# A decoder trunk with product-key expert retrieval: query weights loaded by head, gated one-hot rows in fours of tokens

## The chip, the cores and the metric

One core of a Trainium2 chip runs the whole kernel in one launch. The metric is the device time in microseconds, the median of the runs shown; less is better.

## What is computed

Two residual layers over 256 tokens of width 1024, in float32: a gated short convolution, then a PEER channel mixer; MoBA attention (one block here), then a second PEER mixer. The PEER mixer is what the change touches:

```python
q = (xc @ w_q).reshape(PEER_CHUNK, PEER_HEADS, 2, PEER_HALF)
s1 = jnp.einsum('thd,nd->thn', q[:, :, 0], sub_k1)
s2 = jnp.einsum('thd,nd->thn', q[:, :, 1], sub_k2)
v1, i1 = lax.top_k(s1, PEER_TOPK); v2, i2 = lax.top_k(s2, PEER_TOPK)
...  # the best 16 of the 16 x 16 sums give e_idx; their softmax gives g
a = jax.nn.gelu(jnp.einsum('td,thkd->thk', xc, u_emb[e_idx]), approximate=False)
return jnp.einsum('thk,thkd->td', g * a, v_emb[e_idx])
```

There are 8 heads, 16 experts a head and token, and 128 x 128 experts.

## The kernel before

Instead of gathering, the kernel multiplies every token by all 16,384 rows of `peer_u` (128 items of 128 experts), weighs the gelu of that with a dense matrix of gates, and multiplies by all of `peer_v` (128 items). Each float32 operand is split in two, a rounded part `hi` and a rest `lo`, and three products are summed (hi by `XH`, hi by `XL`, lo by `XH`).

**Items.** All weights come through one line of items (`items`, 512 KB each, numbered over the whole kernel). SP loads an item into one of three `raw` tiles; for a `peer_u` item DVE turns it into `tr` (L145); ACT rounds it to `hi` (L156); POOL takes the difference `lo` in two halves for `peer_u` (L160), DVE mostly for other items; PE multiplies. Every one of `raw`, `tr`, `hi`, `lo` has three buffers, so nothing runs more than three items ahead. `next_item` (L205) writes the preparation of the items ahead first, then item n's matmuls, then side work. The query weights are 8 items of 128 rows each (`wap`, L83): the query of every head is complete only behind the eighth (`mm_wstat`, L423), and is then copied to `qT` in `xbuf` (L736). An U item is 24 matmuls of 256 columns (`u_mm`, L858).

**Side work.** The search and the gates are a list of small steps, each with a cost; behind each item `run_side(budget)` (L167) writes as many as the budget pays (1.62 for a U item). This fixes the order of every engine when the program is built. The list holds: the scores of the queries (L738, PE and a copy by ACT); the top 16 by MAX, MAX_INDEX and MATCH_REPLACE on DVE (L744); the folding of indices; `listed` (L808), which turns the lists; and then, for each of 32 groups of 8 tokens, the dense gates:
- `hots` (L886): DVE compares an iota with the indices and writes two one-hot tiles of 8 tokens (`OH2`, which alternates, and `OH1`);
- `gated` (L891): two DVE instructions multiply `OH1` by the gate's two float16 parts into `OHG`;
- a product (L897): 16 small matmuls (L901) write the 128 x 128 gates of each token to PSUM, two groups deep. `prod()` writes them at the end of the next U item's matmuls, or when the next `gated` or `mult` comes first;
- `mult` (L905): ACT copies the gates of the tiles that come later into `A` (L909), and DVE multiplies the tiles that are done (L911).
`out_pair` (L834) is the gelu of every second U item (ACT, L841 and L849), with a later DVE product (L845) for the tokens whose gates came first. All side work must be written before the last U item (`u_last`).

Below, the U items of a layer are numbered 0 to 127. In the program before, U items 69 to 121 lie beside the groups; this is called the one-hot stage, and U items 0 to 68 the search stage.

Of the kernel before, what the change touches and what calls it, by code (L numbers as in the profile page):

```python
# [21 lines left out]
T = 256  # L22
# [13 lines left out]
def trunk_kernel(ctx: ExitStack, tc, x, norm_mix, norm_ffn, conv_w_in, conv_w, conv_w_out,  # L36
# [29 lines left out]
    OH1, OHG = OH[:, 1], OH[:, 3:5]  # L66
    eT = sb.tile([128, T // TOK, 2, TOK // 2, 2], F16, name="eT")
    gT2 = sb.tile([128, T // TOK, 2, TOK // 2, 2], F16, name="gT2")
# [10 lines left out]
    def scratch(off, n):  # L79
        return big[:, off:off + n]  # L80
# [17 lines left out]
    def peer_items(l):  # L98
        for b in range(8):
            items.append(("w", wap(peer_w_q, l * D, D, 0, b)))  # L100
# [585 lines left out]
    def peer(l):  # L686
        base = 95 * 256
        S = scratch(base, 4096).rearrange("p (b h s n) -> p b h s n", b=2, h=8, s=2)
        qT = xbuf[:, 0:2048].rearrange("p (h t) -> p h t", t=256)
# [23 lines left out]
        U0 = state["use"] + 8  # L713
# [17 lines left out]
        pause(3)  # L731
        add(0.0, keys)
        for b in range(8):
# [21 lines left out]
        n = 0  # L755
        for i in range(2):
            for h in range(0, 8, 2):
                add(0.6, score, i, h, hi4[n % 4])
                n += 1
# [10 lines left out]
        for i in range(2):  # L770
            for h in range(0, 8, 2):
                topk([(S[:, i, h + a, s], v16[:, i, h + a, s], i16[:, i, s, h + a])
                      for a in range(2) for s in range(2)], 0.3)
            add(0.6, dve.tensor_copy, if16[:, i], i16[:, i])
# [45 lines left out]
        gates = lists[2].rearrange("p (s b t) -> p s b t", b=TOK // 2, t=2)  # L820
# [5 lines left out]
        st = {"tiles": 0, "toks": 0, "prod": None, "late": None, "listed": False}  # L826
# [25 lines left out]
        def prod():  # L852
            f, st["prod"] = st["prod"], None
            if f:
                f()
                credit[0] += 1.1

        def u_mm(k):  # L858
            def f(hi, lo):
                bk = lo4[(k // 2) % 4]  # L860
                o = bk[:, (k % 2) * 256:(k % 2) * 256 + 256]
                for b in range(8):
                    s = slice(b * 128, b * 128 + 128)
                    pe.matmul(o, hi[:, s], XH[:, b], start=(b == 0), stop=False)  # L864
                    pe.matmul(o, hi[:, s], XL[:, b], start=False, stop=False)  # L865
                for b in range(8):
                    s = slice(b * 128, b * 128 + 128)
                    pe.matmul(o, lo[:, s], XH[:, b], start=False, stop=(b == 7))  # L868
                if k % 2:
                    out_pair(k // 2, bk)  # L870
                prod()
            return f

        def g_side():
# [16 lines left out]
            def gated(s):  # L891
                prod()
                for a in range(2):
                    dve.tensor_tensor(OHG[:, a], OH1,  # L894
                                      gT2[:, s, a, :, None].to_broadcast([128, TOK // 2, 128, 2]), op=OP.mult)

                def f():  # L897
                    for t in range(TOK):
                        o = hi4[s % 2 * 2 + t // 4][:, t % 4 * 128:t % 4 * 128 + 128]
                        for a in range(2):  # L900
                            pe.matmul(o, OH2[s % 2][:, t // 2, :, t % 2], OHG[:, a, t // 2, :, t % 2],  # L901
                                      start=(a == 0), stop=(a == 1))
                st["prod"] = f

            def mult(s):  # L905
                prod()
                n, t = st["tiles"], slice(s * TOK, s * TOK + TOK)
                if n < NK:
                    act.activation(A[:, n:NK, t], tk(s, n, NK), AF.Copy)  # L909
                w = A[:, 0:n, t]  # L910
                dve.scalar_tensor_tensor(w, tk(s, 0, n), 1.0 / GSC, w, op0=OP.mult, op1=OP.mult)  # L911
                st["toks"] += TOK

            for s in range(NG + 1):
                if s < NG:
                    add(1.25, hots, s)
                    add(1.35, gated, s)
                if s >= 1:
                    add(0.9, mult, s - 1)
# [127 lines left out]
```

## Time and profile before

| | us |
|---|---|
| median of 3 runs (1925.06 to 1937.4) | 1932.14 |
| the profiled execution | 1938.75 |
| its span | 1936.9 |
| TensorE busy in it | 1836.0 |

A row of the trace gives an instruction or a group by its line, engine, operation and tiles; the idle time is that of the engine just ahead of it, with what ended it. PE's weight loads (PEld) lie beside its matmuls.

### The profile page before, as it was taken

To read this page: it belongs to the slowest core of one execution; us is meant where nothing else is said; L and a number is where in the kernel's file an instruction comes from. 1 tells how busy PE (TensorE), PEld (TensorE's weight loads), DVE (VectorE), ACT (ScalarE), POOL (GpSimd) and SP (SyncE) were. 2 spreads that over 40 slices of the span, in tenths; PEclk is the share of its full clock that TensorE was granted. 3 is DMA by queue.
4 is the path that set the end of the run, shared out by engine and by line. 5 is a ranking of instruction groups with operands and counts; after the bars stand their busy time and mean duration, and the time that the engine had idled before them with its cause. 6 is when DMAs were issued, how large, how long until landed. Compare 5 with 4: busy or idle time off the path is not lost.

```text
span 1936.9 us, 32437 instructions
## 1 busy us (share of the span) xinstructions
PE 1836.0 (95%) x12095; PEld 1671.4 (86%) x12095; DVE 1352.6 (70%) x2025; ACT 882.9 (46%) x1143; POOL 840.4 (43%) x561
## 2 busy tenths in 40 slices
PE   7999999888899999999999999998888899999998
PEld 7989999888799888888788799998888898888886
DVE  4757898888987555555554468988889885555555
ACT  4345545433335454544445455454333354544443
POOL 2227999867771000000163368989678720000000
PEclk9999999988999999999899999999899899999999
DMA  6556565534445555665452466654344456566554
GB/s 197 163 183 185 174 189 157 150 110 115 126 123 177 191 194 195 228 192 191 150 172 81 155 180 180 183 176 138 115 121 130 121 171 192 193 194 227 196 191 136
DMA packets 202930, 321.67 MB, mean 166 GB/s; under 512 B 26236, under 2 KB 157844, under 8 KB 202260
## 3 DMA queue, kind: packets, MB, share of 16 engines
q1 hardware_dynamic: 200500, 313.11, 52.7%
q10 hardware_dynamic: 2272, 6.49, 0.9%
q8 instruction: 94, 1.54, 0.3%
q14 instruction: 64, 0.52, 0.1%
HBM read 316.35 MB, written 3.15 MB: 165 GB/s over the span
## 4 chain that ended last, share of the span: by engine, by line
PE 79%; DVE 9%; issue 3%; DMA 3%; POOL 2%; ACT 2%; SPq 1%; DVEq 0%; ACTq 0%; POOLq 0%
PE psum L445 38%; PE psum L864 10%; PE psum L865 10%; PE psum L868 9%; PE psum L432 5%; DVE xbuf L894 4%; PE psum L901 2%; POOL lo L160 2%; DMA raw<-in_peer_u_dram 2%; DVE xbuf L888 2%; DVE tr L145 1%; PE psum L454 1%; PE psum L740 1%; DMA raw<-in_conv_w_out_dram 1%; PE psum L453 1%
## 5 line engine op out<-in xcount | busy, mean ns | idle before, releaser
L160 POOL TENSOR_TENSOR lo<-tr,hi 128x512 fp32r<-128x512 f32 x496 | 736.1, 1517 | 186.7 <-ACT hi L156 186.6
L160 DVE TENSOR_TENSOR lo<-raw,hi 128x1024 fp32r<-128x1024 f32 x298 | 366.3, 1231 | 364.7 <-ACT hi L156 362.8
L156 ACT ACTIVATE hi<-raw 128x1024 fp32r<-128x1024 f32 x336 | 355.6, 1061 | 440.7 <-PE psum L445 343.7
L864 PE MATMUL psum<-xh,hi 128*128 128x256 f32 x2032 | 523.4, 293 | 0.0
L865 PE MATMUL psum<-xl,hi 128*128 128x256 f32 x2032 | 515.7, 290 | 0.0
L445 PE MATMUL psum<-hi,xh 128*128 128x512 f32 x1112 | 431.8, 390 | 0.0
L445 PE MATMUL psum<-hi,xl 128*128 128x512 f32 x1112 | 430.8, 389 | 0.0
L865 PEld LDWEIGHTS psum<-xl,hi 128*128 128x128 f32 x2032 | 404.5, 199 | 0.2
L864 PEld LDWEIGHTS psum<-xh,hi 128*128 128x128 f32 x2032 | 404.2, 199 | 0.2
L145 DVE STREAM_TRANSPOSE tr<-raw 128x1024 f32<-128x1024 f32 x256 | 316.0, 1234 | 75.1 <-POOL lo L160 48.7
L156 ACT ACTIVATE hi<-tr 128x1024 fp32r<-128x1024 f32 x256 | 270.7, 1057 | 182.5 <-DVE tr L145 109.2
L160 POOL TENSOR_TENSOR lo<-raw,hi 128x1024 fp32r<-128x1024 f32 x38 | 92.8, 2456 | 529.9 <-ACT hi L156 521.8
L445 PE MATMUL psum<-lo,xh 128*128 128x512 f32 x1112 | 297.3, 389 | 0.0
L868 PE MATMUL psum<-xh,lo 128*128 128x256 f32 x2032 | 290.6, 285 | 2.2 <-POOL lo L160 2.2
L868 PEld LDWEIGHTS psum<-xh,lo 128*128 128x128 f32 x2032 | 266.5, 195 | 4.3 <-POOL lo L160 4.1
L445 PEld LDWEIGHTS psum<-lo,xh 128*128 128x128 f32 x1112 | 208.7, 188 | 43.5
L445 PEld LDWEIGHTS psum<-hi,xl 128*128 128x128 f32 x1112 | 208.8, 188 | 43.2
L445 PEld LDWEIGHTS psum<-hi,xh 128*128 128x128 f32 x1112 | 208.5, 188 | 42.9
L991 POOL TENSOR_TENSOR big<-xbuf,big 128x256 f32<-128x256 f32 x2 | 1.4, 731 | 363.4 <-DVE rstd L313 363.4
L894 DVE TENSOR_TENSOR xbuf<-xbuf,gT 128x1024 f16<-128x1024 f16 x128 | 143.2, 1157 | 0.9
L901 PE MATMUL psum<-xbuf 128*128 128x128 f16 x1024 | 82.7, 234 | 57.6 <-DVE xbuf L894 57.6
L901 PEld LDWEIGHTS <-xbuf 128*128 128x128 f16 x1024 | 67.2, 104 | 67.0 <-issue 33.1
(154 smaller groups left out, 1500.0 us busy)
## 6 DMA issues: line engine op xcount, KB each, us to landing
raw<-in_peer_u_dram SPq DMA_DIRECT2D x1024, 128.0 KB, 2.9
raw<-in_peer_v_dram SPq DMA_DIRECT2D x256, 512.0 KB, 4.3
raw<-in_conv_w_in_dram SPq DMA_DIRECT2D x96, 128.0 KB, 2.7
raw<-in_attn_w_qkv_dram SPq DMA_DIRECT2D x96, 128.0 KB, 2.6
raw<-in_peer_w_q_dram SPq DMA_DIRECT2D x64, 128.0 KB, 2.7
raw<-in_conv_w_out_dram SPq DMA_DIRECT2D x8, 512.0 KB, 4.3
raw<-in_attn_w_o_dram SPq DMA_DIRECT2D x8, 512.0 KB, 3.7
x_dram<-xbuf ACTq DMA_DIRECT2D x2, 1024.0 KB, 4.6
```

The source lines that it names most:

```text
L145: dve.transpose(TR[m % 3].rearrange("p b (g i) -> p g b i", g=4), RAW[m % 3].rearrange("p (g m) -> p g m", m=256))
L156: act.activation(HI[m % 3], src, AF.Copy)
L160: eng.tensor_sub(LO[m % 3][:, c], src[:, c], HI[m % 3][:, c])
L432: pe.matmul(banks[c // 2][:, (c % 2) * 256:(c % 2) * 256 + 256], w[:, c * 128:c * 128 + 128], xx[:, b], start=(b == 0 and p == 0 and c % 2 ...
L445: pe.matmul(banks[j], x[:, j // 2 * 128:j // 2 * 128 + 128], w[:, j % 2 * 512:j % 2 * 512 + 512], start=(first and p == 0), stop=(last and ...
L453: pe.matmul(banks[j], sl[:, t], hi[:, c], start=False, stop=False)
L864: pe.matmul(o, hi[:, s], XH[:, b], start=(b == 0), stop=False)
L865: pe.matmul(o, hi[:, s], XL[:, b], start=False, stop=False)
L868: pe.matmul(o, lo[:, s], XH[:, b], start=False, stop=(b == 7))
L888: dve.tensor_tensor(OH[:, a:a + 2].rearrange("p a b k t -> p (a b) k t"), iota_t[:, None].to_broadcast([128, TOK, 128, 2]), spread(eT[:, s ...
L894: dve.tensor_tensor(OHG[:, a], OH1, gT2[:, s, a, :, None].to_broadcast([128, TOK // 2, 128, 2]), op=OP.mult)
L901: pe.matmul(o, OH2[s % 2][:, t // 2, :, t % 2], OHG[:, a, t // 2, :, t % 2], start=(a == 0), stop=(a == 1))
```

## The change

- The query weights are loaded by head: an item of kind "q" is 128 columns of all 1024 rows, as 8 runs of 512 bytes for each partition. Its matmuls are those of a U item (`products`, now shared) and give one head's query whole; behind every second one, ACT copies two heads to `qT`, which lies in `big` now.
- The scores of heads h and h+1 may be written behind the query item of head h+2 (`gate=Q0 + h + 3`); scores and top 16 are listed by pairs of heads for both halves of the tokens. The query items have budgets of 2.8 (five) and 1.62 (three), and only one `pause` ahead of `keys`.
- All query items' `lo` is made by POOL.
- `gated` works on four tokens: one instruction writes both parts of the gate, into a ring of three tiles (two in `xbuf`, one new). The work is the same: 64 instructions of 1024 elements.
- The product of four tokens (8 matmuls) is written no sooner than behind the second U item after its `gated`, and not before `mult` has freed its PSUM.
- `mult` is parted: `copied` (ACT) stands two groups behind `hots`, the DVE product three.

```diff
+            elif items[n][0] == "q":
+                l, h = items[n][1]
+                for q in (0, 2, 1, 3):
+                    sp.dma_start(r[32 * q:32 * q + 32].rearrange("p (b c) -> p b c", c=128),
+                                 bass.AP(tensor=peer_w_q.tensor, offset=peer_w_q.offset + (l * D + 256 * q) * D + h * 128,
+                                         ap=[[D, 32], [32 * D, 8], [1, 128]]))
...
+        on_pool.update(range(Q0, U0))
...
-        for b in range(8):
-            next_item(mm_wstat(lo4, b), 1.0)
-        for j in range(4):
-            act.activation(qT[:, 2 * j:2 * j + 2].rearrange("p c t -> p (c t)"), lo4[j], AF.Copy)
+        def q_mm(h):
+            def f(hi, lo):
+                products(lo4[h // 2][:, h % 2 * 256:h % 2 * 256 + 256], hi, lo)
+                if h % 2:
+                    act.activation(qT[:, h - 1:h + 1].rearrange("p h t -> p (h t)"), lo4[h // 2], AF.Copy)
+            return f
...
+        for h in range(0, 8, 2):
+            for i in range(2):
+                add(0.3, score, i, h, hi4[h % 4 + i], gate=Q0 + h + 3)
+            for i in range(2):
                 topk([(S[:, i, h + a, s], v16[:, i, h + a, s], i16[:, i, s, h + a])
                       for a in range(2) for s in range(2)], 0.3)
+        for h in range(H):
+            next_item(q_mm(h), 2.8 if h < H - 3 else 1.62)
...
-        def prod():
-            f, st["prod"] = st["prod"], None
-            if f:
+        def prod(before=NI, last=2 * T):
+            while st["prod"]:
+                n, q, f = st["prod"][0]
+                if n > before or q > last or q // 2 > st["multed"] + 1:
+                    return
+                st["prod"].popleft()
                 f()
-                credit[0] += 1.1
+                credit[0] += 0.45
...
-                prod()
+                prod(state["use"] - 1)
...
+            def gated(q):
+                s, h = q // 2, q % 2
+                prod(last=q - 3)
+                assert len(st["prod"]) < 3
+                g = OHG[q % 3]
+                dve.tensor_tensor(g, OH1[:, None, 2 * h:2 * h + 2].to_broadcast([128, 2, 2, 128, 2]),
+                                  gT2[:, q, :, :, None, :].to_broadcast([128, 2, 2, 128, 2]), op=OP.mult)
...
+            def copied(s):
+                prod(last=2 * s + 1)
+                assert not st["prod"] or st["prod"][0][1] > 2 * s + 1
...
+            def mult(s):
+                n, t = st["copied"].popleft(), slice(s * TOK, s * TOK + TOK)
                 w = A[:, 0:n, t]
                 dve.scalar_tensor_tensor(w, tk(s, 0, n), 1.0 / GSC, w, op0=OP.mult, op1=OP.mult)
...
+            for s in range(NG + 3):
+                if s >= 3:
+                    add(0.9, mult, s - 3)
+                if 2 <= s < NG + 2:
+                    add(0.0, copied, s - 2)
                 if s < NG:
                     add(1.25, hots, s)
+                    add(0.7, gated, 2 * s)
+                    add(0.7, gated, 2 * s + 1)
```

DVE before, from the end of the first layer's normalization (L348) on: `lo` of the query items, then the turns of the first U items, and only then the search (L199).

```order
L348 TENSOR_TENSOR xl<-psum,xh 128x4x128 x4
L160 TENSOR_TENSOR lo_76<-raw_67,hi_73 128x1024
L160 TENSOR_TENSOR lo_77<-raw_68,hi_74 128x1024
L160 TENSOR_TENSOR lo_75<-raw_66,hi_72 128x1024
L160 TENSOR_TENSOR lo_76<-raw_67,hi_73 128x1024
L160 TENSOR_TENSOR lo_77<-raw_68,hi_74 128x1024
L145 STREAM_TRANSPOSE tr_70<-raw_67 128x4x8x32
L160 TENSOR_TENSOR lo_75<-raw_66,hi_72 128x1024
L145 STREAM_TRANSPOSE tr_71<-raw_68 128x4x8x32
```

DVE at the same place now (L356 is the normalization, L207 the search, L153 the turns):

```order
L356 TENSOR_TENSOR xl<-psum,xh 128x4x128 x4
L207 MAX big<-big 128x8 x4
L207 MAX_INDEX big<-big 128x8 x4
L207 MATCH_REPLACE big<-big 128x128 x4
L207 MAX big<-big 128x8 x4
L207 MAX_INDEX big<-big 128x8 x4
L207 MAX big<-big 128x8 x4
L207 MAX_INDEX big<-big 128x8 x2
L153 STREAM_TRANSPOSE tr_70<-raw_67 128x4x8x32
```

The six `lo` are gone from DVE, and 26 search instructions stand ahead of the first turn. Counted through the layer, the first `hots` stands behind 72 turns before and behind 62 now, the 32nd behind 122 and 118. U items 59 to 116 lie beside the groups now: 58 items instead of 53.

DVE in the one-hot stage before, from one turn to the second next `hots` (L888 hots, L894 gated, L911 mult, L845 the later product of a pair):

```order
L145 STREAM_TRANSPOSE tr_71<-raw_68 128x4x8x32
L845 SCALAR_TENSOR_TENSOR big<-psum,big 128x2x8
L911 SCALAR_TENSOR_TENSOR big<-psum,big 128x74x8
L888 TENSOR_TENSOR xbuf<-iota_t,eT 128x2048
L145 STREAM_TRANSPOSE tr_69<-raw_66 128x4x8x32
L894 TENSOR_TENSOR xbuf<-xbuf,gT_85 128x1024 x2
L911 SCALAR_TENSOR_TENSOR big<-psum,big 128x74x8
L145 STREAM_TRANSPOSE tr_70<-raw_67 128x4x8x32
L845 SCALAR_TENSOR_TENSOR big<-psum,big 128x2x16
L888 TENSOR_TENSOR xbuf<-iota_t,eT 128x2048
```

And now (L909 hots, L918 gated, L942 mult, L868 the later product):

```order
L909 TENSOR_TENSOR xbuf<-iota_t,eT 128x2048
L918 TENSOR_TENSOR ohg_84<-xbuf,gT_86 128x1024
L918 TENSOR_TENSOR xbuf<-xbuf,gT_86 128x1024
L153 STREAM_TRANSPOSE tr_69<-raw_66 128x4x8x32
L868 SCALAR_TENSOR_TENSOR big<-psum,big 128x2x16
L942 SCALAR_TENSOR_TENSOR big<-psum,big 128x64x8
L909 TENSOR_TENSOR xbuf<-iota_t,eT 128x2048
L153 STREAM_TRANSPOSE tr_70<-raw_67 128x4x8x32
L918 TENSOR_TENSOR xbuf<-xbuf,gT_86 128x1024
L918 TENSOR_TENSOR ohg_84<-xbuf,gT_86 128x1024
```

The mix is the same; a `mult` belongs to a group three back now, where it was the group just gated.

## Rows read from the trace of the kernel before

**Rows 1.** The page: busy time of the matmuls over the span, and the clock that PE was granted in 40 slices, in tenths of full speed.

```profile
PE 1836.0 (95%) x12095; PEld 1671.4 (86%) x12095; DVE 1352.6 (70%) x2025; ACT 882.9 (46%) x1143; POOL 840.4 (43%) x561
PEclk9999999988999999999899999999899899999999
```

**Rows 2.** Busy time by stretch: the first layer's query items, its search stage, its one-hot stage, and the second layer's one-hot stage. Columns: stretch, its length, busy us and instructions of each engine, PE's clock, share of the DMA engines, GB/s.

```profile
119.89:144.16 24.27, 24.27 (x196) 24.27 (x195) 11.69 (x11) 11.18 (x14) 7.09 (x11) 0.95 0.65 201
144.16:352.85 208.69, 207.60 (x1696) 205.72 (x1695) 172.96 (x497) 108.02 (x130) 186.67 (x139) 1.00 0.62 178
352.85:586.74 233.89, 205.10 (x1786) 200.41 (x1785) 207.55 (x205) 81.17 (x136) 176.98 (x108) 0.91 0.41 121
...
1332.47:1562.86 230.39, 201.53 (x1787) 196.88 (x1786) 207.61 (x205) 80.81 (x136) 177.10 (x108) 0.93 0.41 122
```

**Rows 3.** The timeline of PE (start, length): the first matmul of U items 59, 60, 69 and 122 of the first layer, and of 69 and 122 of the second.

```profile
322.08 0.28 PE L864 MATMUL psum<-xh,hi 128*128 128x256 f32 x1
...
324.96 0.28 PE L864 MATMUL psum<-xh,hi 128*128 128x256 f32 x1
...
352.85 0.28 PE L864 MATMUL psum<-xh,hi 128*128 128x256 f32 x1
...
586.74 0.28 PE L864 MATMUL psum<-xh,hi 128*128 128x256 f32 x1
...
1332.47 0.28 PE L864 MATMUL psum<-xh,hi 128*128 128x256 f32 x1
...
1562.86 0.28 PE L864 MATMUL psum<-xh,hi 128*128 128x256 f32 x1
```

**Rows 4.** Groups of instructions in the first layer's one-hot stage, 352.85 to 586.74: count, busy us, mean ns of one, idle time ahead and what ended it.

```profile
L160 POOL TENSOR_TENSOR lo<-tr,hi 128x512 fp32r<-128x512 f32 x108 | 178.5, 1681 | 56.9 <-ACT hi L156 56.9
...
L894 DVE TENSOR_TENSOR xbuf<-xbuf,gT 128x1024 f16<-128x1024 f16 x64 | 71.6, 1157 | 0.5
L145 DVE STREAM_TRANSPOSE tr<-raw 128x1024 f32<-128x1024 f32 x53 | 65.2, 1231 | 0.0
...
L888 DVE TENSOR_TENSOR xbuf<-iota_t,eT 128x2048 f16<-128x2048 f16 x32 | 44.6, 1393 | 0.0
...
L911 DVE SCALAR_TENSOR_TENSOR big<-psum,big 128x592 f32<-128x592 f32 (+25 forms) x32 | 29.8, 934 | 25.9 <-ACT big L909 25.9
...
L845 DVE SCALAR_TENSOR_TENSOR big<-psum,big 128x16 f32<-128x16 f32 (+23 forms) x24 | 8.8, 366 | 0.0
```

**Rows 5.** Who waited for whom in that stage: us in total, times, longest.

```profile
ACT hi L156 <- DVE tr L145: 37.9, 19, 4.2
PE psum L901 <- DVE xbuf L894: 28.8, 23, 2.2
DVE big L911 <- ACT big L909: 25.9, 10, 4.0
```

**Rows 6.** Two groups of instructions in the second layer's one-hot stage, 1332.47 to 1562.86, with the idle time ahead of them and what ended it (columns as in rows 4).

```profile
L901 PE MATMUL psum<-xbuf 128*128 128x128 f16 x512 | 40.8, 232 | 28.9 <-DVE xbuf L894 28.8
...
L911 DVE SCALAR_TENSOR_TENSOR big<-psum,big 128x592 f32<-128x592 f32 (+25 forms) x32 | 29.8, 934 | 22.3 <-ACT big L909 22.2
```

**Rows 7.** The timeline of DVE and of POOL inside that stage of the first layer: start, length of the piece, and how many instructions it holds.

```profile
399.72 1.73 DVE L888 TENSOR_TENSOR xbuf<-iota_t,eT 128x2048 f16<-128x2048 f16 x1
...
402.66 2.31 DVE L894 TENSOR_TENSOR xbuf<-xbuf,gT 128x1024 f16<-128x1024 f16 x2
...
408.28 1.25 DVE L894 TENSOR_TENSOR xbuf<-xbuf,gT 128x1024 f16<-128x1024 f16 x2
...
415.36 1.22 DVE L888 TENSOR_TENSOR xbuf<-iota_t,eT 128x2048 f16<-128x2048 f16 x1
...
397.65 6.18 POOL L160 TENSOR_TENSOR lo<-tr,hi 128x512 fp32r<-128x512 f32 x4 [0.25 <-ACT hi L156]
...
410.72 2.54 POOL L160 TENSOR_TENSOR lo<-tr,hi 128x512 fp32r<-128x512 f32 x2 [2.37 <-ACT hi L156]
```

**Rows 8.** The timeline of PE around one product at the full clock: 16 small matmuls, then the next U item.

```profile
398.52 1.09 PE L901 MATMUL psum<-xbuf 128*128 128x128 f16 x16
399.42 0.36 PE L864 MATMUL psum<-xh,hi 128*128 128x256 f32 x1
```

**Rows 9.** The timeline at the start of the first layer's query items: all engines, and the load of the keys on ACT's queue.

```profile
119.87 2.12 DVE L348 TENSOR_TENSOR xl<-psum,xh 128x512 fp32r<-128x512 f32 x3 [0.23 <-ACT xh L343]
119.89 2.07 PE L432 MATMUL psum<-xh,hi 128*128 128x256 f32 x8
...
120.86 2.39 POOL L160 TENSOR_TENSOR lo<-raw,hi 128x1024 fp32r<-128x1024 f32 x1 [4.77 <-ACT hi L156]
121.11 0.97 ACTq L724 DMA_DIRECT2D big<-in_peer_k_dram  x1
...
122.93 1.12 PE L432 MATMUL psum<-xl,hi 128*128 128x256 f32 x8
```

**Rows 10.** Loads by tensor: queue, count, KB each, median us from issue to landing.

```profile
raw<-in_peer_u_dram SPq DMA_DIRECT2D x1024, 128.0 KB, 2.9
...
raw<-in_peer_w_q_dram SPq DMA_DIRECT2D x64, 128.0 KB, 2.7
...
big<-in_peer_k_dram ACTq DMA_DIRECT2D x4, 32.0 KB, 4.6
```

More of the change, by code (lines that the diff above doesn't have):

```diff
@@ L65, in trunk_kernel @@
     OH2 = (OH[:, 0], OH[:, 2])
-    OH1, OHG = OH[:, 1], OH[:, 3:5]
+    OH1 = OH[:, 1]
+    ohg2 = sb.tile([128, 2, TOK // 4, 128, 2], F16, name="ohg2")
+    OHG = [OH[:, 3 + i].rearrange("p (a b) k t -> p a b k t", a=2) for i in range(2)] + [ohg2]
     eT = sb.tile([128, T // TOK, 2, TOK // 2, 2], F16, name="eT")
-    gT2 = sb.tile([128, T // TOK, 2, TOK // 2, 2], F16, name="gT2")
+    gT2 = sb.tile([128, T // 4, 2, 2, 2], F16, name="gT2")
     ident = sb.tile([128, 128], F32, name="ident")
@@ L98, in peer_items @@
     def peer_items(l):
-        for b in range(8):
-            items.append(("w", wap(peer_w_q, l * D, D, 0, b)))
+        for h in range(H):
+            items.append(("q", (l, h)))
         for k in range(NK):
@@ L711, in peer @@
         kk = scratch(o, 128)
-        U0 = state["use"] + 8
+        Q0 = state["use"]
+        U0 = Q0 + H
+        on_pool.update(range(Q0, U0))
         V0 = U0 + NK
@@ L730, in keys, with products @@
                 act.activation(kbd[64 * s:64 * s + 64, 128 * s:128 * s + 128], B[7][64 * s:64 * s + 64, 0:128], AF.Copy)
-        pause(3)
+        pause()
         add(0.0, keys)
-        for b in range(8):
-            next_item(mm_wstat(lo4, b), 1.0)
-        for j in range(4):
-            act.activation(qT[:, 2 * j:2 * j + 2].rearrange("p c t -> p (c t)"), lo4[j], AF.Copy)
+        def products(o, hi, lo):
+            for b in range(8):
+                s = slice(b * 128, b * 128 + 128)
+                pe.matmul(o, hi[:, s], XH[:, b], start=(b == 0), stop=False)
+                pe.matmul(o, hi[:, s], XL[:, b], start=False, stop=False)
+            for b in range(8):
+                s = slice(b * 128, b * 128 + 128)
+                pe.matmul(o, lo[:, s], XH[:, b], start=False, stop=(b == 7))
+        def q_mm(h):
[4 more added lines that the diff above has]
+            return f
         def score(i, h, bk):
@@ L753, in topk @@
                         add(cost, dve.match_replace, v, m[:, 0:8], v, NEG)
[L755 to L759, printed above, removed]
         def tables(i):
@@ L818, in listed @@
             act.activation(gT2[:, :, 0], gates, AF.Copy, scale=GSC)
[L820 removed]
+        gates = lists[2].rearrange("p (s b t) -> p s b t", b=2, t=2)
         pause(2)
@@ L861, in f @@
                 o = bk[:, (k % 2) * 256:(k % 2) * 256 + 256]
[L862 to L868, printed above, removed]
+                products(o, hi, lo)
                 if k % 2:
                     out_pair(k // 2, bk)
-                prod()
+                prod(state["use"] - 1)
             return f
@@ L909, in mult @@
                     act.activation(A[:, n:NK, t], tk(s, n, NK), AF.Copy)
+                st["copied"].append(n)
+                st["toks"] += TOK
+            def mult(s):
+                n, t = st["copied"].popleft(), slice(s * TOK, s * TOK + TOK)
                 w = A[:, 0:n, t]
                 dve.scalar_tensor_tensor(w, tk(s, 0, n), 1.0 / GSC, w, op0=OP.mult, op1=OP.mult)
-                st["toks"] += TOK
-            for s in range(NG + 1):
+                st["multed"] += 1
+            for s in range(NG + 3):
[3 more added lines that the diff above has]
+                    add(0.0, copied, s - 2)
                 if s < NG:
                     add(1.25, hots, s)
-                    add(1.35, gated, s)
-                if s >= 1:
-                    add(0.9, mult, s - 1)
+                    add(0.7, gated, 2 * s)
+                    add(0.7, gated, 2 * s + 1)
         add(0.0, st.update, listed=True)
```

23 lines of the change are left out of this document (8 added, 15 removed).

## The prediction, made before the result was known

> **What bounds the kernel now.** I read the page first, then the stretches, then inside the worst stretch the groups, the waits and the timeline. On the page PE is busy 95% of the span [rows 1], so a change of order alone can give back at most about 100 us of idle PE and what the granted clock costs in slices under 9. By stretch [rows 2] both sit in one place: the search stage has PE busy 207.60 of 208.69 us at clock 1.00, while in the two one-hot stages PE stands still 28.8 us each (233.89 less 205.10) and the clock is 0.91 and 0.93. A plain U item takes 2.88 us (324.96 less 322.08 [rows 3]) and a group's 16 small matmuls 0.90 (399.42 less 398.52 [rows 8]). The 53 items and 32 products of the stage would so be 152.6 + 28.8 = 181.4 us of PE; they take 233.89 and 230.39. This gap of some 50 us in each layer is all that is to be had: 28.8 of it is PE's idle time, the rest PE at a lower clock after each stop.
>
> The waits [rows 5, 6] name what stops PE: the product waits for `gated`, 28.8 us in 23 waits, in both layers alike. On DVE the one large wait is `mult` for ACT's copy, 25.9 and 22.2 us; ACT comes late to that copy because it stands behind gelus that wait for PE.
>
> The timeline shows a third thing, which the shares hide. Two halves of `lo` on POOL take 2.54 us when DVE is at something else, so 1.27 each; four take 6.18 us, 1.10 over 4 x 1.27, where a `hots` of 1.73 lies beside them; that `hots` takes 1.22 elsewhere. Two `gated` take 1.25 us alone, and 2.31 where they begin at 402.66 while POOL is still at it until 403.83 [rows 7]. POOL's `lo` and DVE's one-hot instructions therefore take turns. Over the stage POOL's mean is 1681 ns against 1270, and `gated` is 1157 against 625 [rows 4]. I call what they share the port. Its load in the stage before: 53 items by 2.54 (134.6) and 32 groups by 1.25 + 1.22 (79.0), 213.7 us. That is 91% of 233.89 and 93% of 230.39. So PE waits, but a resource behind it is nearly full.
>
> [...]
>
> **The change, part by part.**
>
> *Query weights by head.* In DVE's order the first `hots` moves from behind 72 turns to behind 62. All 128 U items still run, so this gives nothing in the search stage, where PE is full [rows 2]: ten items leave the front, 10 x 2.88 = 28.8 us, and come back behind. What it buys is room: the groups now lie beside 58 items, 59 to 116, not 53, and behind them come 11 plain ones, not 6.
>
> *The one-hot stage.* PE's own work is now 58 x 2.88 + 28.8 = 195.8 us. The product stands an item later than before and a `mult` has a group between itself and its copy, so I take both waits, 28.8 on PE and 25.9 on DVE, as gone. What is late next? DVE: 207.55 us busy now [rows 2], its stops at the port included; five more turns at 1.23 and some later products at 0.37 [rows 4] make some 215. The port: 58 x 2.54 + 79.0 = 226.4. The port is the largest, so I forecast 226.4 us for the stage, at full use. From below: if a one-hot instruction keeps POOL out for only 1.10 of its 1.22 us, the 79.0 are 71 and the stage is 218; with nothing shared it is PE's 195.8. From above: use stays at 91 and 93%, 247.8 and 244.1 us. I take 226.4, since the two waits that made gaps in the port's use are the two that the change moves away, and it lies near the middle of what the rows leave open.
>
> *The form of gated.* 64 instructions of 1024 elements before and after, with two halves of the gate in one; I cost it at nothing. Were it slowed, to 1157 ns each as they are now in the mean, it would add nothing to a DVE row that already holds this.
>
> *Query items.* These 24.27 us have PE busy throughout [rows 2]. Four costs. (a) A head needs all of `XL` in its first 16 matmuls; before, `XL` came in with the third pass at 122.93. The parts are written from 119.87 to 121.99 in three instructions [rows 9]; PE begins at 119.89 and needs the first at its second matmul: 0.7 us late, at most 2.1. (b) POOL makes every `lo` at 2.39 us, under the 2.88 of an item: hidden. If POOL fell behind, PE would wait 0.1 to 0.5 an item. (c) The keys are turned two items earlier. Their load is issued at 121.11, lands some 4.6 us later [rows 9, 10], and PE is there after two items at about 126.8 (the third pass at 122.93, a third of 2.88 for it, and one more item): 0 to 0.7. (d) Runs of 512 bytes make 1024 packets of an item. No row has them in number; runs of 1 KB (U) land in 2.9 us against 2.7 for 4 KB [rows 10], so a lower bound is nothing. From above, a U item's 512 packets hold the DMA engines for 0.62 of 2.88 us at most [rows 2], 1.8 us; twice the packets at no less each take 3.6, 0.7 over an item, 5.6 us for eight. Loads run three items ahead, and 2.9 is the nearer row, so I take little. On SP the count of DMAs stays four an item; ahead of them nothing is moved. Together 1.5 us a layer, from 0 to 8.4. DVE's 26 search instructions ahead of the first turn stand under the U items' slack of three buffers.
>
> **The sum.** In each layer ten plain items leave the front, five go into the stage, five go behind it: saved is 233.89 + 14.4 - 226.4 = 21.9 us, and in the second layer 230.39 + 14.4 - 226.4 = 18.4. Together 40.3, less 3.0 for the query items: 37.3. The profiled execution would go from 1938.75 to 1901.4. It lies 6.6 us above the median of 1932.14, so I forecast 1895 for the median.
>
> **The other ways.**
>
> *PE is the bound.* If POOL and DVE do not really exclude each other, the stage is 195.8 us. Saved: 52.5 + 49.0 - 3.0 = 98.5, 1834. For it: POOL idles 56.9 us of the stage [rows 4] and could take more of its work there. Against it: the stretched rows.
>
> *The gaps stay.* The wait at the product goes, but POOL starves as before, because ACT's `hi` waits for the turn (37.9 us [rows 5]), DVE being in order and late. Use stays at 91 and 93%: saved 0.5 + 0.7 - 3.0, so 1934, no change. For it: DVE is busy 207 of 234 us already and gets more turns; against it: 25.9 us of its idle time go.
>
> *Slower: DVE waits for the ring.* `hots` of a group overwrites rows that the product of two groups back reads, a `gated` a tile of three fours back, and the products now stand later on PE. If DVE arrives first it stops, and behind it stand the turns, so ACT, POOL and PE stop too. One stop of 2.6 us (25.9 in ten, [rows 5]) for every second group is 1.3 us of idle port a group, 41.6 a layer: lost 2 x 41.6 - 37.3 = 45.9, 1978. It turns slower by 1% from 0.88 us a group on (37.3 + 19.3 over 64 groups); before, the port stands idle 0.63 and 0.52. For it: the chain from gate to product and back is longer by one item. Against it: `hots` follows its product by two items or more in the program, and DVE is the late one.
>
> **How the numbers follow.** Port nearly full 0.62; PE the bound or near it 0.13; gaps stay 0.19; ring waits 0.06. One per cent, 19.3 us, is about what a measurement of this kernel can tell from no change; it needs stages of under 235.5 us on the mean. The first two ways are faster: 0.75. The third is the same: 0.19. The last is slower: 0.06. The range goes down to 1865, where the stages are 212, under the 218 of a partly shared port and part of the way to PE's bound, and up to 1928, short of the third way's 1934.
>
> **What would show it.** Right: PE's wait for `gated` under 5 us a layer, DVE's for the copy too; PE now stops at its U matmuls, for POOL's `lo`; POOL and DVE both busy over 90% of a one-hot stage near 226 us; the search in the query items; query items within 3 us of 24.27. Wrong: a stage near 200 us at clock 1.00 (the port is no bound), DVE waiting for small matmuls (ring), POOL idle over 40 us in the stage (the gaps stay), or ACT waiting for `peer_w_q` loads item after item.

## The result and the profile after

Twelve runs of each kernel on one chip: after 1941.03 us in the median (1939.31 to 1943.87), before 1925.63 (1924.85 to 1938.23). The ratio is 1.0065, with a 95% interval of 1.0047 to 1.0082: 0.65% slower, little but clear of the noise, and above the range that was forecast. Before's executions scatter (by 13 us here, by 23 over all sets of runs) and the profiled one (1938.75) lies at the long end; the profiled executions differ by 3.1 us only, and the sums below are made between these.

The page of after: busy times, and PE's clock in 40 slices.

```profile
PE 1823.6 (94%) x12095; PEld 1660.7 (86%) x12095; DVE 1399.5 (72%) x2023; ACT 894.2 (46%) x1149; POOL 866.4 (45%) x573
PEclk9999999999999999999899999999999899999999
```

Against [rows 1], PE has less busy time because its clock sags in fewer slices (0.982 in the mean against 0.973), but DVE has 46.9 us more, from two instructions fewer. The stretches say where. In after the query items end at 147.77, U59 starts at 329.60 and U117 at 571.84, so the third row is the one-hot stage with 58 items; the last row is the second layer's (columns as in [rows 2]).

```profile
119.84:147.77 27.93, 27.78 (x210) 27.09 (x210) 13.64 (x62) 14.01 (x19) 21.79 (x17) 0.95 0.66 195
147.77:329.60 181.83, 177.87 (x1440) 175.74 (x1439) 154.74 (x431) 92.84 (x110) 160.57 (x119) 0.99 0.62 175
329.60:571.84 242.24, 208.25 (x1907) 205.23 (x1905) 240.28 (x214) 93.63 (x148) 189.22 (x118) 0.96 0.43 126
...
1307.26:1551.34 244.08, 209.89 (x1907) 206.99 (x1906) 242.15 (x213) 93.65 (x148) 190.46 (x119) 0.96 0.43 126
```

DVE is busy 240.28 of 242.24 us and 242.15 of 244.08: it has become full, 99%, where it was 89% [rows 2]. The groups of the first layer's stage (columns as in [rows 4]) show on what.

```profile
L168 POOL TENSOR_TENSOR lo<-tr,hi 128x512 fp32r<-128x512 f32 x118 | 190.9, 1646 | 53.0 <-ACT hi L164 52.1 <-ACT psum L864 0.5
L153 DVE STREAM_TRANSPOSE tr<-raw 128x1024 f32<-128x1024 f32 x59 | 72.4, 1228 | 0.0
L918 DVE TENSOR_TENSOR xbuf<-xbuf,gT 128x1024 f16<-128x1024 f16 x43 | 62.9, 1478 | 0.4
L909 DVE TENSOR_TENSOR xbuf<-iota_t,eT 128x2048 f16<-128x2048 f16 x32 | 51.1, 1596 | 0.1
L918 DVE TENSOR_TENSOR ohg<-xbuf,gT 128x1024 f16<-128x1024 f16 x21 | 31.7, 1508 | 0.2
...
L942 DVE SCALAR_TENSOR_TENSOR big<-psum,big 128x528 f32<-128x528 f32 (+28 forms) x32 | 27.8, 870 | 1.2 <-ACT big L935 1.2
```

`gated` (both L918 rows) and `hots` (L909) are as many as before, within the stretch's edges, and take 145.7 us where they took 116.2 [rows 4]: 29.5 us more. Six more turns are 7.2 us, later products 1.2 more, `mult` is 2.0 shorter: 35.9 together, for a rise of DVE's busy time of 32.7 (neighbours overlap a little at their edges in the records, so groups sum to somewhat more). A `gated` went from 1157 to some 1490 ns, a `hots` from 1393 to 1596. The new form of `gated` is not slower by itself: where nothing stops it, it takes 0.66 us (at 405.11 below), and two took 1.25 before [rows 7].

The waits of that stage (columns as in [rows 5]):

```profile
ACT hi L164 <- DVE tr L153: 95.1, 52, 4.9
POOL lo L168 <- ACT hi L164: 52.1, 32, 6.5
...
PE psum L925 <- DVE big L942: 34.0, 20, 5.3
...
DVE big L942 <- ACT big L935: 1.2, 1, 1.2
```

Both waits that the change aimed at [rows 5] are gone: PE no longer waits for `gated`, and DVE's wait for the copy fell from 25.9 to 1.2 us. In their place PE's products wait 34.0 us for `mult` to free PSUM, and ACT waits 95.1 us for turns, where it was 37.9. Both stand in the queue of a full DVE.

Why the stops grew is in the timeline of DVE and POOL (start, length, count), at a place where they meet.

```profile
400.41 1.72 DVE L909 TENSOR_TENSOR xbuf<-iota_t,eT 128x2048 f16<-128x2048 f16 x1
402.16 1.67 DVE L918 TENSOR_TENSOR xbuf<-xbuf,gT 128x1024 f16<-128x1024 f16 x1
...
405.11 0.66 DVE L918 TENSOR_TENSOR ohg<-xbuf,gT 128x1024 f16<-128x1024 f16 x1
...
401.71 3.24 POOL L168 TENSOR_TENSOR lo<-tr,hi 128x512 fp32r<-128x512 f32 x2 [0.67 <-ACT hi L164]
```

POOL's pair of halves comes up at 401.71, while `hots` is at the port until 402.13. POOL, which waits, goes first; the `gated` written right behind `hots` waits out its half and ends at 403.83, 1.67 us for the 0.66 that it takes at 405.11; then POOL's second half runs to 404.95. Counted over both layers, for the 128 `gated` of a kernel, by the DVE instruction directly ahead (stopped: over 1 us; the last column is an experiment below):

```
directly ahead of a gated     before     after      mult between
hots                           6 of 10   36 of 38     2 of 2
another gated                 34 of 64   52 of 52    20 of 28
a turn                         2 of 32    0 of 18     5 of 24
mult, or a later product      20 of 22   13 of 20    32 of 74
mean of a gated, ns              1157      1497        1076
```

Before, a turn stood between `hots` and the first `gated` in 54 of 64 groups. In after, the first `gated` stands directly behind `hots` in 38 groups and the second behind the first in 52, and nearly every such `gated` loses a half of POOL's (88 of 90).

The place alone does not do it: before, the second `gated` always stood behind the first, and 34 of 64 were stopped. What parts the two cases is POOL. The next table counts the one-hot instructions (`gated` and `hots`) directly behind another one, by whether a POOL instruction had begun and not yet ended there (stopped: over 1 us for a `gated`, over 1.5 us for a `hots`; the last two columns are experiments below).

```
stopped, directly behind a one-hot   before     after      mult between   behind turn
a POOL instruction begun              40 of 44   90 of 90   68 of 68       12 of 13
none begun                             0 of 30    0 of 2     1 of 12        0 of 51
```

So a one-hot instruction behind another one is stopped where POOL already has a half to do, and hardly ever otherwise. In after that is nearly always so. Behind any other step it can come up in the middle of a half, and waits out the rest: some 0.5 us in the mean in after, where POOL was at one.

### The profile page after: what moved, and what is told of

It is laid out like the page before. It is cut to its first block, busy times and chain, and to the rows that moved or that the text cites. A ratio compares the mean times of both kernels' runs of the same rounds, so it can differ in the third digit from the quotient of the medians.

```text
span 1939.8 us, 32552 instructions
## 1 busy us (share of the span) xinstructions
PE 1823.6 (94%) x12095; PEld 1660.7 (86%) x12095; DVE 1399.5 (72%) x2023; ACT 894.2 (46%) x1149; POOL 866.4 (45%) x573
## 3 DMA queue, kind: packets, MB, share of 16 engines
q1 hardware_dynamic: 214836, 313.11, 53.4%
## 4 chain that ended last, share of the span: by engine, by line
PE 67%; DVE 16%; issue 6%; DMA 6%; POOL 3%; ACT 1%; SPq 1%; DVEq 0%; ACTq 0%; POOLq 0%
PE psum L453 38%; PE psum L748 7%; PE psum L749 7%; PE psum L752 7%; DMA raw<-in_peer_u_dram 5%; DVE tr L153 5%; DVE xbuf L918 4%; POOL lo L168 3%; PE psum L440 3%; DVE ohg L918 2%; DVE xbuf L909 2%; DVE big L942 1%; SPq L133 1%; DVE big L868 1%; PE psum L462 1%
## 5 line engine op out<-in xcount | busy, mean ns | idle before, releaser
L168 DVE TENSOR_TENSOR lo<-raw,hi 128x1024 fp32r<-128x1024 f32 x286 | 351.7, 1231 | 347.9 <-ACT hi L164 347.3
L748 PE MATMUL psum<-xh,hi 128*128 128x256 f32 x2160 | 550.4, 291 | 0.0
L749 PE MATMUL psum<-xl,hi 128*128 128x256 f32 x2160 | 541.3, 287 | 0.3
L749 PEld LDWEIGHTS psum<-xl,hi 128*128 128x128 f32 x2160 | 423.9, 196 | 1.1 <-DVE xl L356 0.9
L748 PEld LDWEIGHTS psum<-xh,hi 128*128 128x128 f32 x2160 | 423.6, 196 | 0.7 <-ACT xh L351 0.5
L168 POOL TENSOR_TENSOR lo<-raw,hi 128x1024 fp32r<-128x1024 f32 x50 | 121.4, 2442 | 534.1 <-ACT hi L164 528.0
L153 DVE STREAM_TRANSPOSE tr<-raw 128x1024 f32<-128x1024 f32 x256 | 315.5, 1233 | 51.2 <-POOL lo L168 30.1
L752 PE MATMUL psum<-xh,lo 128*128 128x256 f32 x2160 | 308.7, 285 | 7.9 <-POOL lo L168 7.7
L752 PEld LDWEIGHTS psum<-xh,lo 128*128 128x128 f32 x2160 | 281.3, 193 | 11.5 <-POOL lo L168 11.1
L918 DVE TENSOR_TENSOR xbuf<-xbuf,gT 128x1024 f16<-128x1024 f16 x86 | 126.9, 1491 | 0.9
L872 ACT ACTIVATE big<-psum 128x512 f32<-128x512 f32 (+14 forms) x116 | 57.2, 493 | 101.6 <-PE psum L752 99.8
```

The lines of the kernel that those rows point to most:

```text
L153: dve.transpose(TR[m % 3].rearrange("p b (g i) -> p g b i", g=4), RAW[m % 3].rearrange("p (g m) -> p g m", m=256))
L168: eng.tensor_sub(LO[m % 3][:, c], src[:, c], HI[m % 3][:, c])
L872: act.activation(A[:, k:k + 2, n:T], v[:, :, n:T], AF.Gelu)
L918: dve.tensor_tensor(g, OH1[:, None, 2 * h:2 * h + 2].to_broadcast([128, 2, 2, 128, 2]), gT2[:, q, :, :, None, :].to_broadcast([128, 2, 2, ...
```

## The experiments

Each ratio is to before, run on the same chip in the same set.

**Before again.** The kernel before, unchanged, for the scatter.

> The kernel before, unchanged, for a second trace of it: its runs lie at 1925 or at 1932 to 1938 us, and the trace that the prediction was made from is of 1938.75. Theory (DVE is full in the one-hot stage, from stops where it takes turns with POOL): if this run is near 1925, its one-hot stages are shorter by some 6 us each, with fewer or shorter stops of gated (mean under 1157 ns). Rival (something outside the mixers differs): the stages stay at 234 and 230 us and the difference lies elsewhere.

1931.69 us. Its two one-hot stages, 53 items each:

```profile
353.42:576.28 222.86, 193.96 (x1786) 189.13 (x1785) 207.52 (x205) 81.00 (x136) 177.10 (x108) 0.96 0.43 126
1321.92:1555.82 233.90, 205.11 (x1787) 200.43 (x1786) 207.57 (x205) 80.79 (x136) 177.06 (x108) 0.91 0.41 120
```

The same kernel has a stage of 223 us and one of 234, with the same DVE and POOL times; what differs is PE's clock, 0.96 and 0.91, and its busy time, by 11.15 us where the stages differ by 11.04. A `gated` takes 1156 ns in both, so that part of the expectation fell: the scatter is not in the stops. DVE has slack in both, 15 and 26 us; in after's stage it has 2.

**Each half of the change alone.** `query_only`: before with the loads by head and the early search.

```diff
-        for b in range(8):
-            items.append(("w", wap(peer_w_q, l * D, D, 0, b)))
+        for h in range(H):
+            items.append(("q", (l, h)))
...
```

> The kernel before with the query weights by head and the early search alone; gated, product and mult as before. Theory: gated stays in pairs, mean near 1157 ns, the one-hot stage still 53 items and near 232 us, ten items earlier; the search stage is some 4 us a layer longer, as in the changed kernel: 1928 to 1936 us in all. Rival (the query part is what costs): all of the loss is here, 1940 us or more. Second rival (room in the stage is what counts): under 1915.

`ring_only`: before with fours, ring, late product and parted `mult`.

```diff
...
-                    add(1.35, gated, s)
-                if s >= 1:
-                    add(0.9, mult, s - 1)
+                    add(0.7, gated, 2 * s)
+                    add(0.7, gated, 2 * s + 1)
```

> The kernel before with the fours, the ring of three, the late product and the parted mult alone; query weights as before. Theory: gated stands alone between other DVE work and meets POOL each time, mean near 1490 ns against 1157; DVE is busy over 97% of the one-hot stage, which takes 240 us or more for some 58 items: 1930 to 1942 us. Rival (the query part is what costs): 1890 to 1925 us, with gated back under 1200 ns.

`query_only` 1925.68, ratio 0.9985 (0.9954 to 1.0016); `ring_only` 1934.53, 1.0032 (1.0009 to 1.0054). Their first one-hot stages, 53 items in the first and 58 in the second:

```profile
327.52:548.90 221.38, 194.46 (x1786) 189.73 (x1785) 205.11 (x205) 82.96 (x136) 175.50 (x108) 0.96 0.44 126
```

```profile
351.38:595.60 244.22, 210.14 (x1907) 207.13 (x1905) 241.51 (x216) 92.31 (x148) 173.92 (x108) 0.96 0.43 125
```

The full DVE comes with the ring half alone: 241.51 of 244.22 us busy, 6.0 of them `lo` of the last items, which lie in this stage here; `gated` is at 1424 ns in the first layer and 1442 in the second. The query half leaves `gated` at 1139 and costs nothing in the whole that can be measured, though its query items and search stage are longer (see below).

**The two `gated` as one step** (`pair`), so that no other step comes between them.

```diff
-                    add(0.7, gated, 2 * s)
-                    add(0.7, gated, 2 * s + 1)
+                    add(1.4, lambda s=s: (gated(2 * s), gated(2 * s + 1)))
```

> The changed kernel with the two gated of a group written as one side step, so that they stand side by side on DVE; nothing else. Theory: the second of a pair no longer meets POOL, gated's mean goes from 1497 to about 1160 ns, DVE has 20 us less in each one-hot stage, and the stage goes from 242 to some 225 us: 1900 to 1912 us. Rival (the late product and the ring hold the stage): gated changes or not, the stage stays within 4 us of 242 and the time within 8 of 1941.

1920.99, ratio 0.9962 (0.9937 to 0.9987). Groups of its first stage:

```profile
L918 DVE TENSOR_TENSOR xbuf<-xbuf,gT 128x1024 f16<-128x1024 f16 x43 | 61.2, 1444 | 0.0
L909 DVE TENSOR_TENSOR xbuf<-iota_t,eT 128x2048 f16<-128x2048 f16 x32 | 45.7, 1429 | 1.6 <-PE psum L925 1.5
```

A miss: `gated` stays at 1444 ns (1160 was expected), 54 of the 64 second ones of a pair are still stopped, and the time is above the 1900 to 1912 expected. That two `gated` were parted was not the cause. `hots` is shorter, and the stages of 58 items take 235.50 and 233.09 us, which gives 18 of the 20 us against after. This left as cause what stands ahead of a `gated` of either kind: an instruction that holds the port while POOL waits for it.

**POOL's halves made smaller, and less** (`quarter`: four of 256 columns; `halfpool`: two of 256, so half of each `lo` is left out).

```diff
-            for h in range(2 if is_u(m) and eng is pool else 1):
-                c = slice(512 * h, 512 * h + 512) if is_u(m) and eng is pool else slice(0, 1024)
+            for h in range(4 if is_u(m) and eng is pool else 1):
+                c = slice(256 * h, 256 * h + 256) if is_u(m) and eng is pool else slice(0, 1024)
```

> The changed kernel with POOL's lo of an U item in four pieces of 256 columns, not two of 512: the same POOL work, shorter pieces. Theory (DVE is full in the one-hot stage because each one-hot instruction stops for the piece that POOL has begun, and an instruction that stands directly behind another one always does): a stop becomes at most some 0.6 us, not 1.14; gated goes from 1497 to some 1050 ns and hots from 1600 to 1400, DVE has 25 to 35 us less in a stage, and the stage goes from 242 to 215 to 228 us: 1885 to 1915. Rival (the sum of what POOL and DVE ask of the port sets the stage, however it is cut): same sum, stage within 5 us of 242, 1932 to 1945.

> The changed kernel with POOL writing only half of the columns of lo of the U items (two pieces of 256, the other half is left as it was). Theory (DVE's stops at the port fill DVE): POOL asks for half, gated goes under 950 ns, the one-hot stages fall from 242 to 200 to 215 us and come near PE's 196: 1850 to 1885. Rival (the late product and the ring hold the stage): the stages stay over 235 us, 1925 or more.

`quarter` 1922.59, ratio 0.9964 (0.9939 to 0.9989); `halfpool` 1848.51, one run. The stretch over the first stage, of `quarter` and of `halfpool`, and a group of the latter's:

```profile
332.72:560.85 228.13, 212.42 (x1907) 202.54 (x1905) 214.53 (x216) 94.07 (x148) 226.35 (x239) 0.99 0.47 136
```

```profile
322.33:524.01 201.68, 198.86 (x1907) 197.16 (x1906) 194.40 (x213) 91.41 (x148) 108.61 (x117) 1.00 0.52 152
```

```profile
L918 DVE TENSOR_TENSOR xbuf<-xbuf,gT 128x1024 f16<-128x1024 f16 x43 | 39.1, 921 | 5.1 <-PE psum L925 4.7
```

A stop shortens with the piece that it waits out: with quarters `gated` is about 1100 ns, DVE has slack again, and the stages fall to 228.13 and 228.80 us, just past the upper end of what was expected. But POOL is then busy almost without a gap, and the search stage, where POOL also makes `lo`, grows by 5 to 6 us a layer, so the total missed its 1885 to 1915. With half of POOL's work gone, the stages are 201.68 and 204.32 us, 6 and 8.5 above PE's own 195.8, at clock 1.00 and 0.98, and the time is just under the 1850 to 1885 expected. PE's wait for `mult` falls to 2.8 us: it was a sign of the full DVE, not a cause.

**Something else between `hots` and `gated`** (`mult_between`): the same steps, with `mult`, which reads PSUM and one tile, between them.

```diff
-                if s >= 3:
-                    add(0.9, mult, s - 3)
...
                     add(1.25, hots, s)
+                if s >= 3:
+                    add(0.9, mult, s - 3)
+                if s < NG:
                     add(0.7, gated, 2 * s)
```

> The changed kernel with the mult of a group written between its hots and its first gated, not ahead of hots; nothing else. Theory (a one-hot instruction directly behind another one always stops for POOL, since POOL waits for the port and takes it first): the gated that stood behind a hots (38 of 128, 36 of them slow) stands behind a mult now, POOL has its turn beside the mult, gated's mean falls from 1497 to some 1250 to 1350 ns, and the stage from 242 to 228 to 236 us: 1915 to 1932. Rival (what stands ahead of a gated does not matter): gated's mean within 60 ns of 1497, stage within 4 us of 242, 1936 to 1946.

1914.79, ratio 0.9929 (0.9901 to 0.9958), where after has 1.0065: 26 us under after by one step moved. The stretch over its first stage, and two groups in it:

```profile
327.33:559.45 232.12, 206.85 (x1907) 203.98 (x1906) 228.28 (x216) 94.39 (x148) 199.12 (x118) 0.97 0.46 133
```

```profile
L909 DVE TENSOR_TENSOR xbuf<-iota_t,eT 128x2048 f16<-128x2048 f16 x32 | 63.0, 1968 | 2.6
...
L918 DVE TENSOR_TENSOR xbuf<-xbuf,gT 128x1024 f16<-128x1024 f16 x43 | 47.3, 1109 | 0.0
```

`gated` fell by 26 us in the stage, more than expected, and `hots` rose by 12, since it stands directly behind a `gated` now in 50 of 64 groups (47 of them stopped), where it was 2: what POOL does not take from the one it takes in part from the other. The same move in `ring_only`, without the query half (`ring_mult_between`):

> The kernel ring_only (query weights as before) with the edit of mult_between: mult between hots and the first gated. Theory: the order around hots is what costs, with or without the early search, so gated falls from 1430 to some 1080 ns here too and the time from 1934 to 1905 to 1918 us; what then stands between this run and mult_between (1914.8) is the worth of the query part, which I expect within 8 us of nothing. Rival (the fix works only with the room that the early search makes): over 1925 us.

1913.80, ratio 0.9925 (0.9897 to 0.9953). With the order mended, the query half is worth nothing that can be measured (0.9929 with it, 0.9925 without).

**A port step for each item** (`behind_turn`): one U item has turn, `hots`, `mult`, the next turn, `gated`, `gated`, and the later product of a pair behind the step. The groups lie beside 64 items.

```diff
+        state.pop("post", lambda: None)()
...
+                else:
+                    state["post"] = late
...
-                if s >= 3:
-                    add(0.9, mult, s - 3)
...
-                    add(1.25, hots, s)
-                    add(0.7, gated, 2 * s)
-                    add(0.7, gated, 2 * s + 1)
+                    add(0.0, hots, s)
+                if s >= 3:
+                    add(0.0, mult, s - 3)
+                if s < NG:
+                    pause()
+                    add(0.0, gated, 2 * s)
+                    add(0.0, gated, 2 * s + 1)
+                    pause()
```

> The changed kernel with the order of the one-hot stage fixed item by item: behind a turn stands a hots and then a mult, behind the next turn the two gated of the group and then a later product, so that never a one-hot instruction stands directly behind a hots and each group gets two U items. Theory: behind a turn POOL mostly waits for ACT's hi of that turn, so the port is free; hots falls to 1250 ns and gated to 900 or less, DVE is no longer full, and a stage of 64 items takes some 225 to 245 us (port load 64 x 2.54 + 79 = 242; PE 213), where the changed kernel takes 242 + 6 x 2.88 = 260 for the same items: 1880 to 1915. Rival (order does not matter, only the load): gated stays over 1350 ns and the time over 1925.

1879.21 (1878.37 to 1879.93), ratio 0.9734 (0.9687 to 0.9781): faster than before and, by the ratios, than after; the best of all that compute the whole. The stretch over its first stage of 64 items, two groups in it, and the timeline of DVE and POOL at a meeting:

```profile
328.34:558.62 230.28, 220.45 (x2050) 216.61 (x2049) 226.93 (x221) 97.60 (x159) 180.67 (x129) 1.00 0.50 147
```

```profile
L912 DVE TENSOR_TENSOR xbuf<-iota_t,eT 128x2048 f16<-128x2048 f16 x31 | 62.4, 2014 | 0.0
L921 DVE TENSOR_TENSOR xbuf<-xbuf,gT 128x1024 f16<-128x1024 f16 x43 | 40.0, 951 | 0.0
```

```profile
446.77 2.11 DVE L912 TENSOR_TENSOR xbuf<-iota_t,eT 128x2048 f16<-128x2048 f16 x1
...
450.78 1.13 DVE L921 TENSOR_TENSOR xbuf<-xbuf,gT 128x1024 f16<-128x1024 f16 x1
451.84 0.68 DVE L921 TENSOR_TENSOR ohg<-xbuf,gT 128x1024 f16<-128x1024 f16 x1
...
445.00 2.81 POOL L168 TENSOR_TENSOR lo<-tr,hi 128x512 fp32r<-128x512 f32 x2 [0.76 <-ACT hi L164]
```

`gated` is at 951 and 977 ns, but `hots` at 2014, where 1250 was expected: it now comes up while POOL is at its pair, waits until 447.81, and has another 1.07 us behind that. The two `gated` still stand together in every group; only 12 of the 64 second ones are stopped, since POOL mostly has nothing to do there. DVE is still 98.5% busy, though even so the clock is 1.00 and PE stands still less than 10 us. Two ways to relieve DVE or the port further:

`behind_turn_dve4`: the `lo` of every fourth item of the stage on DVE.

```diff
+        on_dve.update(range(U0 + 62, V0 - 4, 4))
```

> The kernel behind_turn with lo of every fourth U item of the one-hot stage made by DVE in one piece (1.23 us) and not by POOL (2.54). Theory: if the port is the bound in behind_turn, it has 16 x 1.31 = 21 us less to do in a stage and the time falls by 15 to 35 us more; if DVE is still the bound there, DVE gets 16 x 1.23 = 20 us more and the time rises by 20 to 40 us.

`behind_turn_quarter`: `lo` in quarters, in the one-hot stage alone.

```diff
...
+            w = 1024 if eng is dve or not is_u(m) else 256 if m in in_stage else 512
+            for h in range(1024 // w):
...
```

> The kernel behind_turn with POOL's lo in four pieces of 256 columns for the U items of the one-hot stage alone. Theory (DVE is still 98.7% busy in that stage, 27 us of it stops of hots and 20 of gated, and a stop ends with POOL's piece): the stops halve, the stage of 64 items goes from 231 to 220 to 228 us, PE's own 213 not far: 1860 to 1876. Rival (POOL, which was 100% busy in four pieces, is the bound then): stage 231 us or more, 1878 to 1895.

Both are slower than `behind_turn`: 1909.18, ratio 0.9888 (0.9840 to 0.9937), with DVE busy 244.07 of 246.41 us in its stage; and 1897.17, 0.9824 (0.9769 to 0.9879), with POOL full, as the stretch over its stage shows:

```profile
330.15:568.29 238.14, 230.69 (x2050) 217.55 (x2049) 210.16 (x220) 96.95 (x159) 237.46 (x255) 1.00 0.48 142
```

In `behind_turn` DVE was nearly full and POOL busy 180.67 of 230.28 us. The first run gave 18.8 us of `lo` to the full DVE, and the time rose by 30 us, as expected for that case. In the second the stops did shorten, and DVE was busy 16.8 us less, but POOL's quarters filled POOL: the rival.

**What takes the port** (`onex2`): each `gated` as two instructions of 512 elements whose operands run with a step of two, token by token; these pieces were meant to run at half the rate that a `gated` has in after, which the expectation calls double speed.

```diff
...
+                for a in range(2):
+                    dve.tensor_tensor(g[:, a].rearrange("p b k t -> p b t k"),
+                                      OH1[:, 2 * h:2 * h + 2].rearrange("p b k t -> p b t k"),
+                                      gT2[:, q, a, :, :, None].to_broadcast([128, 2, 2, 128]), op=OP.mult)
```

> [...] First reading (any DVE instruction with two operands in SBUF takes the port): the pieces still meet POOL, their mean is 0.9 to 1.2 us, DVE has 10 to 60 us more in a stage, which is 250 us or more: 1955 to 2050. Second reading (only instructions at double speed take the port): the pieces take 0.6 us each whatever POOL does (1.2 a gated against 1.50), POOL's lo beside them is not stretched, and the stage falls to 215 to 230 us: 1890 to 1920.

2073.86, one run: the pieces still meet POOL, as the first reading has it, but their mean and the time lie beyond the ranges given. Part of its first stage's pieces:

```profile
L919 DVE TENSOR_TENSOR xbuf<-xbuf,gT 128x512 f16<-128x512 f16 x80 | 104.5, 1371 | 0.4
```

A piece of 512 elements takes 0.69 to 0.73 us where POOL is idle, about as long as 1024 elements of a `gated` in after (0.66), so at about half the rate, and 1371 ns in the mean: it is stopped at half the rate too, and the second reading fell. That any DVE instruction with two operands in SBUF takes the port, as the first reading has it, is more than these pieces show.

## Why the prediction was wrong

- **The step that failed** is DVE in the one-hot stage: "207.55 us busy now [rows 2], its stops at the port included; five more turns at 1.23 and some later products at 0.37 [rows 4] make some 215", and with it, for `gated`, "I cost it at nothing". The stops were carried over as if they belonged to the instruction. They belong to what stands ahead of it while POOL has a half to do. DVE measured 240.28 us where 215 was forecast, since `hots` and `gated` are 29.5 longer, and so it, not the port's 226.4, set the stage (242.24). That the form itself costs nothing was right; its new place does. `ring_only` shows it without the query half, `mult_between` takes half of it back by one moved step. Both orders stand ahead of the prediction, and the new one shows `hots` with two `gated` directly behind it; what was read from them is that the mix is the same.
- **The port's load** as the bound, 226.4 us, came out wrong in use: 226.4 of 242.24 is 93%, as before. In time this is the way called "the gaps stay" (247.8 and 244.1 against 242.24 and 244.08), and in most of its mechanism too: POOL idles 53.0 us, over the 40 that the prediction named as that way's sign, and is busy 78% of the stage, because ACT waits 95.1 us for turns of a late DVE. What that way lacked is why DVE is late: it took the stops as unchanged, and they grew, so that its time nearly fits is in part luck. Nor is the load a floor: `behind_turn` does 64 items in 230.28 us, where the same terms add to 64 x 2.54 + 79.0 = 241.6. The terms count every half and every one-hot instruction whole; no run shows that they keep each other out for all of that time, and added up so they are some 11 us too much here. How much of a half of POOL's is not exclusive was not measured; that a stop is some 1.1 us, where a half takes 1.27 alone, points to an estimated 0.17.
- **That the port matters** was right: PE alone as the bound (1834) is not quite reached even with POOL's work halved (`halfpool`, 1848.51). So was the aim: both waits went. Neither was worth time, since DVE came last instead.
- **Query items.** 27.93 against 24.27 us, within the 3 us of the forecast only if one counts that four of the eight scores moved there; they are 3.43 us of PE work. 24.26 became 28.51 in the second layer. So the loads by head cost some 0.2 and 0.8 us, for 1.5 each forecast: right in size. The landing of these loads stayed at 2.7 us, with the packets that were expected: the queue has 214,836 where it had 200,500, 896 more for each of the 16 items.
- **The search stage** was held to be unchanged. By the front as a whole (query items and search, less ten items of 2.88 us), 5.6 and 5.0 us were lost. It comes with the query half: `query_only` loses 5.6 and 4.4 there. PE waits 3.8 us for POOL's `lo` in five waits of the first layer's search stage in after; the rest was not followed.
- **The ring** did not stop DVE: in after's stage DVE waits for small matmuls less than 1 us.
- **The bill** between the profiled executions: stages 6.1 and 0.7 us won (233.89 and 230.39, with 14.4 for the five items more, against 242.24 and 244.08), fronts 5.6 and 5.0 lost: 3.8 us slower, 3.1 measured. Against before's median the loss is 15.4 us, because most of its executions are shorter than the profiled one: it has one-hot stages of 223 us as well as of 234. After's twelve lie within 4.6 us.

That a waiting POOL is served ahead of the next DVE instruction is read from the timelines and the counts; no run shows the arbitration itself. Why before's stage has two lengths at the same DVE time stays open; PE's clock differs with them (0.96 and 0.91 in `before_again`), and what moves it was not followed. In the first one-hot stage of the profiled before it is 0.50 for eight spells of 3.4 or 6.8 us, 44.4 together, and 1.00 between them. Each spell begins in a stop of PE or within 0.6 us behind one, but the stops of 1.45 us that end at 362.65 and 368.98 have none, so the prediction's "after each stop" says more than the trace.

## What to carry to other kernels

The time of an instruction that shares a resource is a property of the order, not of the instruction: when a change alters what stands directly ahead of it, take its free time and its stops apart and count the stops anew. Put vector instructions that hold the shared port where the other engine has nothing waiting for it: a `gated` takes 951 to 977 ns so in `behind_turn`, against 1478 to 1508 in after. A step that does not hold the port between two that do (in these stages a half of `lo` took 1.29 us in before and after where only turns and products from PSUM lay beside it, against 1.74 and 1.68 beside one-hot instructions, and a turn 1.23 with a half beside it or without) helps only in part: in `mult_between` 12 of the 26 us that `gated` gained came back as longer `hots`, while in `behind_turn`, where each port step has an item of its own, two `gated` stand together and are mostly not stopped. An engine at 89% with stops in its busy time is not an engine with slack.

## What the runs showed of the hardware

A one-hot instruction directly behind another is passed by a POOL instruction that waits there (90 of 90 in after, 40 of 44 before, 68 of 68 in `mult_between`, 12 of 13 in `behind_turn`), and goes at once where none waits (0 of 2, 0 of 30, 1 of 12 and 0 of 51 stopped). A stop is about 1.1 us for a half of `lo` that takes 1.27 alone; smaller POOL pieces shorten the stop (1102 ns a `gated` with quarters against some 1490) but cost POOL more: 995 ns each, stops included, so 1990 for the 512 columns that take 1646 in after.
